# Opening of the kernel: three issuing queues, sums of squares on TensorE, one joint root, first step 512 wide

## The chip, the cores and the metric

The kernel runs on one core of a Trainium2 chip. The metric is the device time of one execution in microseconds: 1518.89 us before, the median of 3 runs (1516.44 to 1520.34). A profiled execution took 1518.84 us, of which the profile's span covers 1517.1 us. All times in the texts below count from the start of that span.

## The reference

A two-layer backbone block. There are two token streams of 256 tokens each, 1024 channels wide: the latents x and the context ctx. What the change touches is the very beginning of layer 0:

```python
mod_x = (jax.nn.silu(c) @ w_mod[l] + b_mod[l])[:, None, :]
mod_c = (jax.nn.silu(c_ctx) @ w_mod[l] + b_mod[l])[None, None, :]
hc = _modulate(xc, g_pre_mix[l], sc1, cc1)
h = _modulate(x, g_pre_mix[l], sx1, cx1)
proj = h @ w_in
# _modulate(x, g, shift, scale) = _rms_norm(x, g) * (1 + scale) + shift
# _rms_norm(x, g) = x * rsqrt(mean(x * x) + EPS) * g
```

So each token needs the sum of its 1024 squares and a reciprocal root, each channel needs a shift and a scale that come from a product of the conditioning vector with `w_mod`, and then the projections begin. All else (Fourier mixing, two attentions, a convolution, gates, the MLP, and layer 1) follows on these results and isn't changed.

## The kernel before, in words

Activations are held channel-major: x is eight tiles of 128 channels x 512 tokens, stream 0 (the latents) in columns 0 to 255 and stream 1 (the context) in columns 256 to 511. A matrix product in full precision is done as three passes over parts: each operand is split into a high part (a cast, on ACT) and a low part (a subtraction, on DVE), and `mm3` (L147) issues high x high (L149), high x low (L150) and low x high (L151).

The opening of layer 0 is `conv_proj` (L760). It takes eight steps, one per block k of 128 input channels, and in each step six output tiles (six PSUM banks: four "mm", one "tp", one "o") take 3 matmuls each, 18 in all, 512 columns wide from step 1 on (`wide`, L748). Step k needs the modulated block k of both streams (`entry`, L1236, and `modulate_tile`, L362: a multiply on DVE, L367, the high part on ACT, L132, the low part on DVE, L133), its weights (`raw`, 384 KB, loaded by SP and split at L126 and L127), and the shifts and scales of block k. These come from `mods_pe` (L246): a load of 1 MB (`boot`, a ring of six tiles), sixteen matmuls at L256, a copy on ACT (L259), four small matmuls at L261 and an addition on DVE (L264). Block k+2 is done behind step k.

Step 0 has a function of its own, `start` (L1211). For each stream in turn it squares eight x tiles on ACT (L1220) and adds them up on DVE (L1222), sums over the partitions with products against a column of ones on PE (`rstd_add`, L317), takes the root on DVE with Newton steps (`rsqrt_cols`, L175), spreads it over the partitions with products against the identity on PE (`rstd_rows`, L359) and copies the result to SBUF. Stream 0's root, modulation and half of step 0 (256 columns) come first; then those of stream 1.

The loads of the opening are issued in `load_x` (L230) from SP's queue, in this order: stream 0's eight x tiles, the first block of `w_mod`, two tables, the first weights, stream 1's eight x tiles. Two more tables are issued from ACT's queue in `setup` (L186). One DMA completes on one of a few semaphores that are taken in turn, so a later issue can wait for an earlier landing.

The order of instructions on each engine is fixed before the run by a planner. It goes by priorities and by estimated times: work within `high_priority` goes ahead, and work that is ready by its estimate can be put ahead of older work that isn't.

Of the kernel before, what the change touches and what calls it, by code (L numbers as in the profile page):

```python
# [9 lines left out]
F = mybir.dt.float32  # L10
R = mybir.dt.float32r
I32 = mybir.dt.int32
BF = mybir.dt.bfloat16
AF = mybir.ActivationFunctionType
ALU = mybir.AluOpType
AX = mybir.AxisListType
ORDER = mybir.DependencyInfo(mybir.DependencyClass.NoSync, mybir.DependencyReason.DATA)
PSUM = bass.MemoryType.PSUM

P = 128  # L20
D = 1024
KT = 8
L = 256
T = 512
DEPTH = 2
EPS = 1e-6
# [9 lines left out]
C_COS, C_SIN, C_ID, C_ONE = 0, 256, 512, 640  # L36
C_HSEL = 768
C_RSEL = 770
NCONST = C_RSEL + 2
# [41 lines left out]
class Body:  # L81
# [20 lines left out]
    def new(self, name, shape, dtype=F, pool=None, space=None):  # L102
        if space is not None:
            pool = getattr(self, "psum", None)
            if pool is None:
                pool = self.psum = self.ec(self.tc.tile_pool(name="psum", bufs=1, space=PSUM))
        return (pool or self.const).tile(shape, dtype, tag=name, name=name)
# [39 lines left out]
    def mm3(self, out, w, x, start, stop, shared=False):  # L147
        nc = self.nc
        i = nc.tensor.matmul(out, w[0], x[0], start=start, stop=False, skip_group_check=shared)  # L149
        nc.tensor.matmul(out, w[0], x[1], start=False, stop=False, skip_group_check=shared)  # L150
        nc.tensor.matmul(out, w[1], x[0], start=False, stop=stop, skip_group_check=shared)  # L151
        return i

    def mms(self, out, passes, start, stop):
        for i, (w, x) in enumerate(passes):
            self.nc.tensor.matmul(out[:w.shape[-1]], w, x, start=start and i == 0, stop=stop and i == len(passes) - 1)  # L156
# [26 lines left out]
            for o, q, h in cols:  # L183
                self.hold = nc.vector.scalar_tensor_tensor(o, q, 1.5, o, ALU.add, ALU.mult).ins.name

    def setup(self):  # L186
        nc, a, new = self.nc, self.a, self.new
        c = self.consts = new("consts", [P, NCONST])
        ccol, th = new("ccol", [P, KT, 2]), new("cth", [P, KT, 2])
        nc.scalar.dma_start(ccol, a["ccol"])  # L190
        nc.scalar.dma_start(c[:, C_ID:], a["consts"][:, C_ID:])
        self.cos, self.sin = c[:, C_COS:C_COS + L], c[:, C_SIN:C_SIN + L]
        self.ident, self.ones = c[:, C_ID:C_ID + P], c[:, C_ONE:C_ONE + P]
        self.hsel = c[:, C_HSEL:C_HSEL + 2]
        self.rsel = c[:, C_RSEL:C_RSEL + 2]
        nc.scalar.activation(th, ccol, AF.Tanh, scale=0.5)
        self.scol = new("scol", [P, KT, 32])
        nc.vector.memset(self.scol, 0.0)
        nc.vector.scalar_tensor_tensor(th, th, 1.0, ccol, ALU.add, ALU.mult)
        nc.vector.tensor_scalar(self.scol[:, :, 0:2], th, 0.5, None, ALU.mult)  # L200

        self.mods = new("mods", [P, DEPTH, 48, 2])
        self.coef = new("coef", [P, DEPTH, 4, KT, 2])
        self.st4 = self.ring("st4", 16, [P, 4])
        self.st8 = [new(f"st8_{i}", [P, 8]) for i in range(4)]
        self.st32 = [new(f"st32_{i}", [P, 32]) for i in range(4)]
# [20 lines left out]
        for l in range(DEPTH):  # L227
            nc.vector.tensor_scalar(self.dwh[:, l], self.vec[:, l, V_DW:V_DW + 3 * TAPS].rearrange("p (j t) -> p j t", j=3), 0.5, None, ALU.mult)

    def load_x(self):  # L230
        self.vec = self.new("vecs", [P, DEPTH, NVEC])
        self.bmod = self.new("bmod", [P, DEPTH, 48])
        with self.tc.high_priority(WPRIO):
            for k in range(KT):
                self.nc.sync.dma_start(self.x[k][:, :L], self.a["xT"][0, k])
            self.first = {0: self.boot()}
            self.nc.sync.dma_start(self.first[0], self.a["wmod0"][0])
            self.nc.sync.dma_start(self.bmod, self.a["bmod"])
            self.nc.sync.dma_start(self.vec, self.a["vecs"])
            raw0 = self.raw()[:, :768]  # L240
            self.nc.sync.dma_start(raw0, self.a["wuc"][0, 0])
            for k in range(KT):
                self.nc.sync.dma_start(self.x[k][:, L:], self.a["xT"][1, k])
        return raw0

    def mods_pe(self, c):  # L246
# [651 lines left out]
    def attention_part(self, l, n):  # L898
        tc = self.tc
        ns = self.ns = n // L  # L900
        if l == 0:
            with tc.tile_pool(name="boot", bufs=1, reuse_waits="tile") as pool:
                self.boot = self.ring("boot", 6, [P, 2 * D], F, pool)
                raw0 = self.load_x()
                self.setup()
                cbanks = self.conv_proj(l, n, raw0)
            self.setup_late()
        else:
            cbanks = self.conv_proj(l, n)
        with ExitStack() as ctx:  # L910
            pool = ctx.enter_context(tc.tile_pool(name=f"mix{l}", bufs=1, reuse_waits="tile"))
            new = lambda name, shape, dtype=F: self.new(f"{name}", shape, dtype, pool)
# [25 lines left out]
            banks = [self.ps() for _ in range(4)]  # L938
# [151 lines left out]
            for s in range(ns):  # L1090
                sl = slice(s * L, (s + 1) * L)
                acc = self.stat(l)
# [116 lines left out]
                self.chain = self.norm_step(l, 3, ya, acc, s, 1.0 / D, None, (l + 1, 0), "mm")  # L1209

    def start(self, banks, raw0):  # L1211
        self.rs0 = self.tmp("l")
        sls = [slice(s * L, (s + 1) * L) for s in range(2)]
        two = []
        for s in range(2):
            acc = self.rstd_bank(L, "s" if s else "o")
            sm = self.tmp("l")[:, :L]
            for k in range(KT):
                sq = self.tmp("g")[:, :L] if k else sm
                self.nc.scalar.activation(sq, self.x[k][:, sls[s]], AF.Square)  # L1220
                if k:
                    self.nc.vector.tensor_tensor(sm, sm, sq, op=ALU.add)  # L1222
            self.rstd_add(acc, sm, 0, 0)
            two.append(self.rstd_sum(acc, L, 1.0 / D))
            if s == 0:
                self.mods_pe(0)
                self.nc.scalar.copy(self.rs0[:, sls[0]], self.rstd_rows(*two[0], L))
                self.entry(0, (0,))
                w = self.chunk(raw0, (1, 768), first=False)
                self.mods_pe(1)  # L1230
        self.wide(None, self.h, sls[0], banks, 0, w)
        self.nc.scalar.copy(self.rs0[:, sls[1]], self.rstd_rows(*two[1], L))
        self.entry(0, (1,), False)
        self.wide(None, self.h, sls[1], banks, 0, w)

    def entry(self, k, streams, coefs=True):  # L1236
        if coefs:
            self.coefs(0, 0, k, k + 1)
        for s in streams:
            self.modulate_tile(0, 0, s, k, self.rs0[:, s * L:(s + 1) * L])  # L1240

# [43 lines left out]
WPRIO = 4000  # L1285
# [104 lines left out]
```

## Time and profile before

| | |
|---|---|
| median of 3 runs | 1518.89 us |
| profiled execution | 1518.84 us |
| its span | 1517.1 us |
| TensorE (PE) busy | 1454.5 us, 96% |
| VectorE (DVE) busy | 1192.3 us, 79% |
| ScalarE (ACT) busy | 802.5 us, 53% |
| GpSimd (POOL) busy | 123.0 us, 8% |
| one x tile of one stream | 128 KB, 16 of them |
| one block of `w_mod` (boot) | 1024 KB |
| weights of one step (raw) | 384 KB |
| tables consts, vecs, bmod, ccol | 130, 137, 48 and 8 KB |

The page gives each engine's busy time, then the span in 40 slices with a digit for the busy tenths of each, then the chain of work that ended last. In a row of a timeline the first number is the start in us, the second the duration, then engine, line, operation, what is written and read, and the count; in brackets stands the idle time before it and what ended it. A name that ends in q is an engine's queue, which issues DMAs. Rows that merge several instructions give the stretch that they cover.

### The profile page before, as it was taken

What the parts mean: (1) busy time and instruction counts of PE and PEld (TensorE: products, weight loads), DVE (VectorE), ACT (ScalarE), POOL (GpSimd) and SP (SyncE); (2) the same over time, 40 slices, a digit from 0 to 9 for tenths busy, and PEclk for the clock granted to TensorE, in tenths of its full rate; (3) what the DMA queues carried; (4) which work ended last, traced back from release to release, by engine and by line L of the source; (5) the groups of instructions that cost most, each with busy time, mean ns of one, the idle gap of its engine ahead of it and who ended that gap; (6) DMA issues with size and microseconds to landing.
All of it is one profiled execution on the core that took longest, in us unless ns stands there. A gap on an engine that the chain in (4) does not pass through costs nothing.

```text
span 1517.1 us, 25021 instructions
## 1 busy us (share of the span) xinstructions
PE 1454.5 (96%) x9242; PEld 1297.4 (86%) x9242; DVE 1192.3 (79%) x2689; ACT 802.5 (53%) x1584; POOL 123.0 (8%) x165
## 2 busy tenths in 40 slices
PE   5999999999999999899999999989998999899997
PEld 4787788878787899898889999978798999899886
DVE  5699998888889959748975577889998976675565
ACT  3334665555554346753443335553775775577643
POOL 0100000002121002201110011120000110000000
PEclk9999999999999999999999999999999999999999
DMA  8522222413335554666776565362232445466552
GB/s 310 163 71 80 67 66 67 139 56 125 113 122 156 181 181 141 233 196 209 242 254 196 181 223 181 112 214 73 86 108 84 140 132 177 130 203 196 168 191 98
DMA packets 74010, 230.02 MB, mean 152 GB/s; under 512 B 8480, under 2 KB 17184, under 8 KB 72608
## 3 DMA queue, kind: packets, MB, share of 16 engines
q1 hardware_dynamic: 60192, 181.10, 37.1%
q0 software_dynamic: 13408, 47.19, 9.6%
q8 instruction: 72, 1.18, 0.3%
q14 instruction: 50, 0.41, 0.1%
q10 hardware_dynamic: 288, 0.14, 0.0%
HBM read 227.35 MB, written 1.05 MB: 151 GB/s over the span
## 4 chain that ended last, share of the span: by engine, by line
PE 79%; DVE 10%; ACT 4%; DMA 3%; issue 2%; POOL 0%; SPq 0%; DVEq 0%; ACTq 0%; POOLq 0%
PE ps_mm L149 20%; PE ps_mm L150 19%; PE ps_mm L151 19%; PE ps_s L438 3%; DVE wl L127 2%; PE ps_s L156 2%; PE ps_tp L438 1%; PE ps_o L438 1%; PE ps_tp L550 1%; ACT wh L126 1%; PE ps_o L156 1%; PE ps_s L149 1%; PE ps_s L150 1%; PE ps_s L151 1%; PE ps_o L150 1%
## 5 line engine op out<-in xcount | busy, mean ns | idle before, releaser
L126 ACT CAST wh<-raw 128x1024 fp32r<-128x1024 f32 (+3 forms) x283 | 259.9, 919 | 312.7 <-PE ps_mm L150 168.3
L127 DVE TENSOR_TENSOR wl<-raw,wh 128x1024 fp32r<-128x1024 f32 (+3 forms) x283 | 304.7, 1078 | 137.5 <-ACT wh L126 135.4
L149 PE MATMUL ps_mm<-h,wh 128*128 128x512 f32 (+2 forms) x996 | 344.4, 348 | 8.1 <-ACT h L132 3.9
L151 PE MATMUL ps_mm<-h,wl 128*128 128x512 f32 (+2 forms) x996 | 345.1, 347 | 4.7 <-DVE wl L127 4.5
L150 PE MATMUL ps_mm<-h,wh 128*128 128x512 f32 (+2 forms) x996 | 343.5, 345 | 0.0
L149 PEld LDWEIGHTS ps_mm<-h,wh 128*128 128x128 f32 x996 | 190.0, 192 | 32.4 <-ACT h L132 4.1
L151 PEld LDWEIGHTS ps_mm<-h,wl 128*128 128x128 f32 x996 | 191.1, 192 | 29.3 <-DVE wl L127 7.9
L150 PEld LDWEIGHTS ps_mm<-h,wh 128*128 128x128 f32 x996 | 191.0, 192 | 21.8 <-issue 0.8
L127 DVE TENSOR_TENSOR wlx<-raw,whx 128x1024 fp32r<-128x1024 f32 (+2 forms) x85 | 93.9, 1106 | 34.6 <-ACT whx L126 34.4
L799 DVE SCALAR_TENSOR_TENSOR cy<-cv,half_dw,cy 128x512 f32<-128x512 f32 (+1 forms) x180 | 102.7, 610 | 0.2
L149 PE MATMUL ps_mm<-h,whx 128*128 128x256 f32 (+2 forms) x336 | 98.4, 294 | 4.3 <-ACT tf L516 2.5
L126 ACT CAST whx<-raw 128x1024 fp32r<-128x1024 f32 (+2 forms) x85 | 80.9, 953 | 40.9 <-PE ps_mm L150 19.9
L287 DVE SCALAR_TENSOR_TENSOR tl<-wm,srow 128x1024 bf16<-128x1024 f32 x80 | 97.6, 1220 | 0.8
L150 PE MATMUL ps_mm<-h,whx 128*128 128x256 f32 (+2 forms) x336 | 97.9, 292 | 0.0
L151 PE MATMUL ps_mm<-h,wlx 128*128 128x256 f32 (+2 forms) x336 | 97.0, 292 | 0.0
L151 PE MATMUL ps_mm<-r,wl 128*128 128x256 f32 (+1 forms) x260 | 86.3, 332 | 1.6 <-DVE wl L127 1.6
L149 PE MATMUL ps_mm<-r,wh 128*128 128x256 f32 (+1 forms) x260 | 86.5, 333 | 0.1
L150 PE MATMUL ps_mm<-r,wh 128*128 128x256 f32 (+1 forms) x260 | 86.0, 331 | 0.0
L126 ACT CAST hs<-hid 128x256 fp32r<-128x256 f32 x96 | 38.6, 407 | 70.9 <-PE ps_o L438 39.5
L149 PEld LDWEIGHTS ps_mm<-h,whx 128*128 128x128 f32 x336 | 63.8, 190 | 6.3 <-ACT tf L516 2.7
L127 DVE TENSOR_TENSOR hs<-hid,hs 128x256 fp32r<-128x256 f32 x96 | 41.8, 439 | 34.5 <-ACT hs L126 33.9
L855 POOL TENSOR_TENSOR x<-x,tg 128x512 f32<-128x512 f32 (+1 forms) x32 | 36.8, 1149 | 354.9 <-DVE tg L853 293.8
(398 smaller groups left out, 3538.7 us busy)
## 6 DMA issues: line engine op xcount, KB each, us to landing
raw<-in_wff SPq DMA_DIRECT2D x135, 512.0 KB, 4.2
raw<-in_wcol SPq DMA_DIRECT2D x88, 512.0 KB, 3.5
wm<-in_wmodT POOLq DMA_DIRECT2D x56, 512.0 KB, 4.1
wmg<-in_wmodT POOLq DMA_DIRECT2D x24, 512.0 KB, 3.8
raw<-in_wout SPq DMA_DIRECT2D x24, 512.0 KB, 3.9
boot<-in_wmod SPq DMA_DIRECT2D x8, 1024.0 KB, 7.4
raw<-in_wuc SPq DMA_DIRECT2D x16, 384.0 KB, 3.3
raw<-in_wdv SPq DMA_DIRECT2D x8, 512.0 KB, 3.7
```

The costliest lines, as they stand in the source:

```text
L126: nc.scalar.copy(hi, src)
L127: return nc.vector.tensor_tensor(lo, src, hi.bitcast(F), op=ALU.subtract)
L149: i = nc.tensor.matmul(out, w[0], x[0], start=start, stop=False, skip_group_check=shared)
L150: nc.tensor.matmul(out, w[0], x[1], start=False, stop=False, skip_group_check=shared)
L151: nc.tensor.matmul(out, w[1], x[0], start=False, stop=stop, skip_group_check=shared)
L156: self.nc.tensor.matmul(out[:w.shape[-1]], w, x, start=start and i == 0, stop=stop and i == len(passes) - 1)
L287: i = nc.vector.scalar_tensor_tensor(self.junk, w, 1.0, self.srow[:, s, :], ALU.mult, ALU.mult, accum_out=self.mods[:, l, c, s:s + 1])
L438: self.nc.tensor.matmul(banks[t][i][:, c], x[q][:, tok], w[j][:, a:b], start=start and j + q == 0, stop=stop and q == 1, skip_group_check= ...
L550: nc.tensor.transpose(ps[:, i * P:(i + 1) * P], p[:, i * P:(i + 1) * P], self.ident)
L799: nc.vector.scalar_tensor_tensor(y3, src, w, y3, ALU.mult, ALU.add)
L855: eng.tensor_tensor(mg, mg, th, op=ALU.add)
```

## The change

The loads go out from three queues: stream 0's x tiles, then the weights, from SP; stream 1's x tiles from POOL; the tables and the first block of `w_mod` from ACT. Squares of stream 0 are taken on ACT, those of stream 1 on DVE, and nothing is added up there: each squared tile goes to PE, where products against the column of ones accumulate over the eight tiles in four columns of one PSUM bank, two for each stream. One root is taken for all four columns, spread over 512 columns and copied once; then both streams are modulated and step 0 is done 512 wide. PE also gets fourteen matmuls of 512 columns on a zeroed bfloat16 tile whose result nobody reads: six at the beginning and one behind the sums of each k. The small tiles of the setup move to the pool of the opening, and the setup's four small operations get a high priority.

```diff
+    def load_x(self, pool):
+        nc = self.nc
...
         with self.tc.high_priority(WPRIO):
+            nc.gpsimd.memset(self.warm, 0.0)
+            self.first = {0: self.boot()}
+            nc.scalar.dma_start(self.ccol, self.a["ccol"])
+            nc.scalar.dma_start(self.consts[:, C_ID:], self.a["consts"][:, C_ID:])
+            nc.scalar.dma_start(self.bmod, self.a["bmod"])
+            nc.scalar.dma_start(self.vec, self.a["vecs"])
+            nc.scalar.dma_start(self.first[0], self.a["wmod0"][0])
             for k in range(KT):
-                self.nc.sync.dma_start(self.x[k][:, :L], self.a["xT"][0, k])
-            self.first = {0: self.boot()}
-            self.nc.sync.dma_start(self.first[0], self.a["wmod0"][0])
-            self.nc.sync.dma_start(self.bmod, self.a["bmod"])
-            self.nc.sync.dma_start(self.vec, self.a["vecs"])
+                nc.sync.dma_start(self.x[k][:, :L], self.a["xT"][0, k])
+            for k in range(KT):
+                nc.gpsimd.dma_start(self.x[k][:, L:], self.a["xT"][1, k])
             raw0 = self.raw()[:, :768]
-            self.nc.sync.dma_start(raw0, self.a["wuc"][0, 0])
-            for k in range(KT):
-                self.nc.sync.dma_start(self.x[k][:, L:], self.a["xT"][1, k])
+            nc.sync.dma_start(raw0, self.a["wuc"][0, 0])
...
     def start(self, banks, raw0):
+        nc = self.nc
         self.rs0 = self.tmp("l")
-        sls = [slice(s * L, (s + 1) * L) for s in range(2)]
-        two = []
-        for s in range(2):
-            acc = self.rstd_bank(L, "s" if s else "o")
-            sm = self.tmp("l")[:, :L]
+        junk, bank, out = self.ps("s"), self.ps("o"), self.ps("tp")
+        sums = bank[:, T - 4:]
+
+        def keep_warm():
+            nc.tensor.matmul(junk, self.warm[:, :P], self.warm, start=True, stop=True)
+
+        for i in range(6):
+            keep_warm()
+        head = None
+        with self.tc.high_priority(2 * WPRIO):
             for k in range(KT):
-                sq = self.tmp("g")[:, :L] if k else sm
-                self.nc.scalar.activation(sq, self.x[k][:, sls[s]], AF.Square)
-                if k:
-                    self.nc.vector.tensor_tensor(sm, sm, sq, op=ALU.add)
-            self.rstd_add(acc, sm, 0, 0)
-            two.append(self.rstd_sum(acc, L, 1.0 / D))
-            if s == 0:
-                self.mods_pe(0)
-                self.nc.scalar.copy(self.rs0[:, sls[0]], self.rstd_rows(*two[0], L))
-                self.entry(0, (0,))
-                w = self.chunk(raw0, (1, 768), first=False)
-                self.mods_pe(1)
-        self.wide(None, self.h, sls[0], banks, 0, w)
-        self.nc.scalar.copy(self.rs0[:, sls[1]], self.rstd_rows(*two[1], L))
-        self.entry(0, (1,), False)
-        self.wide(None, self.h, sls[1], banks, 0, w)
+                for s in range(2):
+                    x = self.x[k][:, s * L:(s + 1) * L]
+                    sq = self.tmp("fa"[s])[:, :L]
+                    if s == 0:
+                        nc.scalar.activation(sq, x, AF.Square)
+                    else:
+                        nc.vector.tensor_tensor(sq, x, x, op=ALU.mult)
+                    for t in range(2):
+                        i = nc.tensor.matmul(sums[:, 2 * s + t:2 * s + t + 1], sq[:, t * P:(t + 1) * P], self.ones[:, 0:1],
+                                             start=head is None, stop=k == KT - 1, skip_group_check=True)
...
+                keep_warm()
+        self.mods_pe(0)
+        v, r, q, h = (self.st4() for _ in range(4))
+        nc.vector.tensor_scalar(v, sums, 1.0 / D, EPS, ALU.mult, ALU.add)
+        self.rsqrt(r, v, q, h)
+        nc.scalar.copy(self.rs0, self.rstd_rows(out, r, T))
+        self.entry(0, range(2))
+        w = self.chunk(raw0, (1, 768), first=False)
+        self.mods_pe(1)
+        self.wide(None, self.h, slice(0, T), banks, 0, w)
```

`rsqrt` (L166) is the root that is now called: two operations, then three times three, each on all columns at once.

## Rows read from the trace of the kernel before

**Rows 1.** The page: busy time of the engines; busy tenths of the DMA engines.

```profile
PE 1454.5 (96%) x9242; PEld 1297.4 (86%) x9242; DVE 1192.3 (79%) x2689; ACT 802.5 (53%) x1584; POOL 123.0 (8%) x165
...
DMA  8522222413335554666776565362232445466552
```

**Rows 2.** The chain that ended last, its first 36 us: start, duration, what.

```profile
4.50 7.79 DMA boot<-in_wmod
12.32 1.98 PE ps_s L256 x16
...
20.21 0.21 PE ps_mm L150
...
31.35 0.12 PE ps_mm L151
...
33.41 0.43 PE ps_mm L149
```

**Rows 3.** Timeline: DMA issues on SP's queue, and later ones on POOL's.

```profile
6.55 7.58 SPq L243 DMA_DIRECT2D x<-in_xT  x8
...
13.80 0.33 SPq L243 DMA_DIRECT2D x<-in_xT  x1
...
62.79 2.13 POOL L708 DMA_DIRECT2D r<-in_csl  x4 [9.38 <-PE ps_s L256]
```

**Rows 4.** DMA issues (count, size, us to landing), and a wait of SP's queue.

```profile
x<-in_xT SPq DMA_DIRECT2D x1, 128.0 KB, 2.7
...
r<-in_csl POOLq DMA_DIRECT2D x4, 256.0 KB, 4.5
...
SPq L243 <- DMA boot<-in_wmod: 2.0, 1, 2.0
```

**Rows 5.** Stretches: length, busy time per engine, granted clock, DMA share, GB/s.

```profile
2.00:14.00 12.00, 2.69 (x20) 1.51 (x20) 5.69 (x29) 4.31 (x10) 0.00 (x0) 1.00 0.90 280
10.00:12.00 2.00, 0.00 (x0) 0.00 (x0) 1.78 (x15) 0.00 (x0) 0.00 (x0) 1.00 0.95 352
...
24.00:28.00 4.00, 2.15 (x21) 1.37 (x14) 2.87 (x18) 1.43 (x4) 0.00 (x0) 0.97 1.00 407
28.00:31.00 3.00, 3.00 (x11) 1.97 (x12) 2.33 (x5) 1.45 (x3) 0.00 (x0) 0.50 1.05 430
...
38.13:43.94 5.81, 5.81 (x40) 4.16 (x39) 3.40 (x9) 2.02 (x4) 0.00 (x0) 1.00 0.69 250
```

**Rows 6.** Timeline: products of the root, of a steady step, of a block.

```profile
14.19 1.22 PE L359 MATMUL ps_o<-consts,st 128*128 128x128 f32 x4
...
22.57 0.85 PE L317 MATMUL ps_s<-consts,tl 128*128 128x1 f32 x4
...
25.30 0.71 PE L359 MATMUL ps_s<-consts,st 128*128 128x128 f32 x4 [0.41 <-DVE st L184]
...
34.75 0.35 DVE L264 TENSOR_SCALAR mods<-ps_s,bmod 128x2 f32<-128x2 f32 x2 [4.31 <-PE ps_s L261]
...
39.13 0.50 PE L149 MATMUL ps_mm<-h,wh 128*128 128x512 f32 x1
...
43.94 1.07 PE L256 MATMUL ps_s<-boot,scol 128*32 128x256 f32 x16
```

**Rows 7.** Timeline: DVE and ACT operations that the sum is made from.

```profile
4.35 0.42 DVE L1222 TENSOR_TENSOR tl<-tl,tg 128x256 f32<-128x256 f32 x1 [0.60 <-ACT tg L1220]
...
9.94 0.16 DVE L327 TENSOR_SCALAR st<-ps_o 128x2 f32<-128x2 f32 x1 [1.11 <-PE ps_o L317]
...
11.58 0.28 DVE L184 SCALAR_TENSOR_TENSOR st<-st,st 128x1 f32<-128x1 f32 x2
...
35.33 0.88 DVE L367 SCALAR_TENSOR_TENSOR ta<-x,coef,tl 128x256 f32<-128x256 f32 x2
...
35.85 0.91 ACT L132 ACTIVATE h<-ta,mods 128x256 fp32r<-128x256 f32 x2 [2.01 <-DVE ta L367]
...
70.07 0.60 ACT L782 ACTIVATE tf<-ps_mm 128x512 f32<-128x512 f32 x1 [2.13 <-PE ps_mm L151]
```

More of the change, by code (lines that the diff above doesn't have):

```diff
@@ L184, in rsqrt_cols, with setup @@
                 self.hold = nc.vector.scalar_tensor_tensor(o, q, 1.5, o, ALU.add, ALU.mult).ins.name
-    def setup(self):
+    def setup(self, pool):
         nc, a, new = self.nc, self.a, self.new
[L188 to L191, printed above, removed]
+        c, ccol = self.consts, self.ccol
+        th = new("cth", [P, KT, 2], F, pool)
         self.cos, self.sin = c[:, C_COS:C_COS + L], c[:, C_SIN:C_SIN + L]
@@ L195, in setup @@
         self.rsel = c[:, C_RSEL:C_RSEL + 2]
[L196 to L200, printed above, removed]
+        with self.tc.high_priority(2 * WPRIO):
+            nc.scalar.activation(th, ccol, AF.Tanh, scale=0.5)
+            self.scol = new("scol", [P, KT, 32], F, pool)
+            nc.vector.memset(self.scol, 0.0)
+            nc.vector.scalar_tensor_tensor(th, th, 1.0, ccol, ALU.add, ALU.mult)
+            nc.vector.tensor_scalar(self.scol[:, :, 0:2], th, 0.5, None, ALU.mult)
         self.mods = new("mods", [P, DEPTH, 48, 2])
@@ L228, in setup_late @@
             nc.vector.tensor_scalar(self.dwh[:, l], self.vec[:, l, V_DW:V_DW + 3 * TAPS].rearrange("p (j t) -> p j t", j=3), 0.5, None, ALU.mult)
-    def load_x(self):
+    def load_x(self, pool):
+        nc = self.nc
         self.vec = self.new("vecs", [P, DEPTH, NVEC])
         self.bmod = self.new("bmod", [P, DEPTH, 48])
+        self.consts = self.new("consts", [P, NCONST])
+        self.ccol = self.new("ccol", [P, KT, 2], F, pool)
+        self.warm = self.new("warm", [P, T], BF, pool)
         with self.tc.high_priority(WPRIO):
-            for k in range(KT):
-                self.nc.sync.dma_start(self.x[k][:, :L], self.a["xT"][0, k])
-            self.first = {0: self.boot()}
-            self.nc.sync.dma_start(self.first[0], self.a["wmod0"][0])
-            self.nc.sync.dma_start(self.bmod, self.a["bmod"])
-            self.nc.sync.dma_start(self.vec, self.a["vecs"])
+            nc.gpsimd.memset(self.warm, 0.0)
[5 more added lines that the diff above has]
+            nc.scalar.dma_start(self.first[0], self.a["wmod0"][0])
+            for k in range(KT):
+                nc.sync.dma_start(self.x[k][:, :L], self.a["xT"][0, k])
+            for k in range(KT):
+                nc.gpsimd.dma_start(self.x[k][:, L:], self.a["xT"][1, k])
             raw0 = self.raw()[:, :768]
-            self.nc.sync.dma_start(raw0, self.a["wuc"][0, 0])
-            for k in range(KT):
-                self.nc.sync.dma_start(self.x[k][:, L:], self.a["xT"][1, k])
+            nc.sync.dma_start(raw0, self.a["wuc"][0, 0])
         return raw0
@@ L903, in attention_part @@
                 self.boot = self.ring("boot", 6, [P, 2 * D], F, pool)
-                raw0 = self.load_x()
-                self.setup()
+                raw0 = self.load_x(pool)
+                self.setup(pool)
                 cbanks = self.conv_proj(l, n, raw0)
@@ L1231, in start @@
-        self.wide(None, self.h, sls[0], banks, 0, w)
-        self.nc.scalar.copy(self.rs0[:, sls[1]], self.rstd_rows(*two[1], L))
-        self.entry(0, (1,), False)
-        self.wide(None, self.h, sls[1], banks, 0, w)
-    def entry(self, k, streams, coefs=True):
-        if coefs:
-            self.coefs(0, 0, k, k + 1)
+        junk, bank, out = self.ps("s"), self.ps("o"), self.ps("tp")
+        sums = bank[:, T - 4:]
+        def keep_warm():
+            nc.tensor.matmul(junk, self.warm[:, :P], self.warm, start=True, stop=True)
@@ new lines, in start @@
+        for i in range(6):
+            keep_warm()
+        head = None
+        with self.tc.high_priority(2 * WPRIO):
+            for k in range(KT):
+                for s in range(2):
[8 more added lines that the diff above has]
+                                             start=head is None, stop=k == KT - 1, skip_group_check=True)
+                        if head is not None and k == 0:
+                            self.tc.add_manual_dep(i.ins, head, ORDER, reason="bank clear first")
+                        head = head or i.ins.name
+                keep_warm()
@@ L1239, in entry @@
+        self.mods_pe(0)
[7 more added lines that the diff above has]
+        self.wide(None, self.h, slice(0, T), banks, 0, w)
+    def entry(self, k, streams):
+        self.coefs(0, 0, k, k + 1)
         for s in streams:
```

## The prediction

> **What bounds the kernel now.** I read the page first, then the chain of waits of the first 36 us, then the table of stretches, then single instructions there. Over the whole span TensorE is busy 96% and the DMA engines are mostly not [rows 1]; only in the first slice are they at 8 tenths. So a microsecond won at the opening is won at the end, if the first dense step starts earlier and nothing starves it after. What I follow is one mark: the start of the second projection step, at 33.41 in the chain [rows 2]. From there on a step takes 5.81 us of PE without a gap (38.13 to 43.94, PE busy 5.81 of them) with 250 GB/s of transfers beside it, less than the 352 and 407 of earlier stretches [rows 5]. Later steps are copies of this one, so whatever moves the mark moves the end.
>
> The chain up to the mark [rows 2]: the first modulation block (1 MB) is issued behind eight x tiles at 4.50 and takes 7.79; its products begin at 12.32; around 20 PE does step 0 for stream 0 alone, the sums of stream 1 wait behind it (22.57) [rows 6], a second root follows, and stream 1's half of step 0 runs from 28 on. There the granted clock reads 0.50, the level of 1.2 GHz, after a stretch 24 to 28 in which PE had 2.15 us of work [rows 5]. The clock column reads 1.00 before that, but matmuls of 256 columns start 0.21 apart at 20.21 and 0.12 apart at 31.35 [rows 2]; I go by the spacing and take PE as running at half speed until about 23.
>
> **The change part by part.** Sum against the profiled execution: 1518.84 us, of which 1517.1 is the span; the median of the three runs is 1518.89, so the two are interchangeable.
>
> *Loads.* Before, SP issues all 16 x tiles, stream 1 behind the block: its eight issues take 7.58 us [rows 3], one of them held 2.0 us by the block's landing [rows 4]. The last x tile is issued at 13.80 and lands 2.7 later, at 16.5 [rows 3, 4]. Now stream 1 goes out from POOL, whose issues cost 0.53 each (2.13 for four) [rows 3], eight done by about 5.5; nothing else that the opening needs stands on POOL. Needed before the last sum: x 2.10 MB, the block 1.05, small tables 0.33, in all 3.48 MB, since the three queues run at once and the block on ACT's queue takes its share. Between 2 and 14 us the transfers ran at 280 GB/s [rows 5]: 2 + 12.4 = 14.4 us for the last x tile. Below: at 352 (10 to 12 us) 11.9. Above: if SP's next loads (0.39 and 1.05 MB) pass a lagging stream 1, 4.92 MB, 19.6.
>
> *Sums of squares.* The additions on DVE go (14 of about 0.43, [rows 7]), DVE squares stream 1 instead. Squares of the last tile 0.43, its two one-column products 0.85 (22.57) [rows 6]: 15.7. ACT's squares of stream 0 run three tiles ahead and are hidden as long as x arrives slower than 0.43 per tile, which 14.4 says.
>
> *The joint root.* Before, 1.92 us for two columns (9.94 to 11.86) [rows 7]. Now twelve instructions, one behind the other; dependent ones start 0.19 to 0.20 apart there: 2.2. To 17.9. The first modulation block's products (1.07 to 1.98) are hidden under it; if they weren't, see rival C.
>
> *Rows of the root.* Four products instead of two: 0.71 at the fast and 1.22 at the slow spacing for two [rows 6], so 1.2 to 2.1; I take 1.5, to 19.4. The copy to SBUF is 512 wide, 0.60 as a like copy [rows 7]: 20.0. Then both streams' modulation, as in a steady step from 35.33 to 36.76, 1.43 [rows 7]: PE can start step 0 at 21.4.
>
> *Step 0, 512 wide.* A steady step without the block behind it is 39.13 to 43.94, 4.8, four small products of the block before it included [rows 6], which stand here too. The engine comes to it from a thin stretch like that of 24 to 28; before, 3.1 us passed at half speed then [rows 5], which would cost half of that, 1.6; with the extra products in the gap I take 0.8. To 27.0. The next block's products take 1.0 [rows 6], so the mark is at 28.0 instead of 33.4: a gain of 5.4.
>
> *Added and hidden.* Fourteen warming products (512 columns, some 0.21 to 0.43 each, from the spacings above doubled) stand in PE while it waits for x. Without that cover, they would cost up to 8 x 0.43 = 3.4, and this is in rival D. The memset of their operand costs POOL well below one DMA issue. Tables moved to other queues land earlier, which nobody waits for.
>
> *What is late next.* The second block follows on SP behind x and the first weights: 4.92 MB is through by 19.6 at 280 GB/s, before step 0 starts at 21.4. The third follows 1.44 MB later, 3.5 us at 407 and 5.1 at 280, so at 24.7 at the latest, and is wanted at 27.0. So no transfer takes over the path.
>
> A rule that speaks against the change: the Trainium skill, "DMA: Bandwidth & Descriptors", section "Issuing engines are not separate DMA queues", says that transfers started from several engines share the same 16 DMA engines and interleave, so that spreading them saves only issue time. The trace agrees so far as the mean busy share was already 0.90 between 2 and 14 us with nearly everything on SP [rows 5]; its result is rival A.
>
> Sum: 1518.84 - 5.4 = 1513.4 us.
>
> **Rivals.**
>
> A. *The transfer isn't won.* Stream 1 on POOL is overtaken by what SP issues after its own x tiles; the last x lands at 19.6, 5.2 later than forecast, gain 0.2: 1518.6. For it: DMA share 0.90, and large rows beside 1 KB rows; POOL's transfers of 256 KB took 4.5 us to land [rows 4]. Against: both x queues are issued within a microsecond of each other. The same page, section "Queues, rings and completion order", has every DMA engine go round the queues packet by packet, which would make this worse with larger packets; no row here shows packets of three queues at once.
>
> B. *More is won.* Transfers reach 352 GB/s (11.9, 2.5 earlier), and the warming products keep PE at the fast level: sums 0.35 less, rows 0.3 less, step 0 0.8 less. Gain 5.4 + 2.5 + 0.65 + 0.8 = 9.4: 1509.4. For it: 352 and 407 GB/s were reached once larger rows were in flight; against: x rows alone ran near 280 and below.
>
> C. *The planner puts the first block's chain ahead of the root* on DVE, as it is written before it. Then the root waits for the block's products, 1.07, and from their end to that of the addition, 1.7 (33.41 to 35.10) [rows 2, 6], with projection products in between; of these 2.8 I take 2.2, gain 3.2: 1515.6. Before, it reordered freely by readiness, which speaks against.
>
> D. *Slower: sums bound by PE at half speed.* A tile pair costs four one-column products (twice 0.85) and one warming product 0.43: 2.1 us. From about 5 us, eight take until 22.1, against 15.7; rows 2.1 (0.6 more); step 0 starts at half speed for 3.1 us (0.7 more than counted): 7.7 lost against the forecast, 1521.1; with all of step 0 (18 x 0.43, 2.1 more than counted) and its block (1.98, 0.9 more) at half speed 10.0 lost, 1523.4. It decides when the sums end after 15.7 + 5.4 = 21.1. For it: PE worked nearly gap-free from 12.32 to about 16 and still had the slow spacing at 20.21 [rows 2]. Against: the dense work from 28 on [rows 5] brought the fast spacing by 31.35 [rows 2].
>
> **How the numbers follow.** Forecast 0.42 (own range 1511 to 1516), A 0.15, B 0.23, C 0.10, D 0.10. Some 0.3% (4.6 us) is what a measurement can tell from no change. Faster by more: 0.28 of the forecast, which stands only 0.8 beyond that bound, all of B, 0.02 of C: 0.53. Slower by more: 0.07 of D and 0.02 of A, whose upper end I don't know: 0.09. The rest, 0.38, within. The range reaches from just below B to past A, 1508.5 to 1520.0, and leaves out D and a little of B.
>
> **What would show it.** Right: last x tile landed by 13 to 16 us; the root's first instruction near 15.7; step 0's first product of 512 columns near 21.4; step 1's at 26 to 30, and the same 5.81 us steps after. Loads wrong: the wait before the last squares is on x and ends near 19 (A) or near 12 (B). Order wrong: DVE's first modulation addition stands ahead of the root (C). Clock wrong: sums packed without a gap at 2 us per tile pair, the granted clock at 0.50 in step 0 (D). The whole prediction fails if steps after the second are no longer 5.81 us, or if the gain at the mark is there and isn't at the end.

## The result and the profile after

The kernel after takes 1530.28 us (median of 6 runs, 1526.66 to 1531.12), the kernel before beside it 1519.12 (6 runs): ratio 1.0077, 95% interval 1.0058 to 1.0095. It is slower, where 1513.4 was forecast. The profiled execution took 1530.87 us, its span 1529.0. The mark (start of step 1), 33.41 in the chain of before [rows 2], is at 43.08 in the chain after, 9.7 us later instead of 5.4 earlier. So most of the 11.9 us between the two spans arises in the opening.

First the page of the kernel after, engines and DMA; it answers to [rows 1]:

```profile
PE 1475.6 (97%) x9294; PEld 1311.9 (86%) x9294; DVE 1189.3 (78%) x2665; ACT 799.0 (52%) x1575; POOL 129.0 (8%) x174
...
DMA  7432222322444554766776565362223445466552
```

TensorE has 21.1 us more busy time than before (1454.5), and 18.1 of it stand ahead of the mark: 35.74 us busy up to 42.94, before 17.67 up to 33.34. Of these, 6.05 are the warming products, which ran while TensorE had nothing else to do. The chain of waits after shows most of the rest (start, duration, what; it answers to [rows 2]):

```profile
3.11 9.05 DMA boot<-in_wmod
...
12.30 1.03 PE ps_s L262 x2
13.33 1.80 PE ps_o L1239 x8
15.13 1.01 PE ps_s L262 x8
16.14 3.50 PE ps_o L1239 x16
19.64 1.00 PE ps_s L262 x6
20.64 6.92 PE ps_o L1239 x32
27.56 0.99 PE ps_s L262 x2
28.55 0.95 PE ps_s L267 x4
29.49 1.89 PE ps_s L262 x14
...
31.89 1.03 PE ps_s L267 x4
...
33.76 2.09 PE ps_tp L365 x8
...
38.04 1.20 PE ps_mm L149 x4
...
43.08 0.35 PE ps_mm L149
```

This is to be read from the top. L262 are the products of the first modulation block, L1239 the one-column products of the sums. The chain does not begin at x. It begins at the first block (1 MB), which lands at 12.16, and the one-column products follow it: 1.80 + 3.50 + 6.92 = 12.2 us of them, with 3.0 us of block products between. The sums end at 27.56.

The timeline after, TensorE and then VectorE (start, duration, engine, line, operation; in brackets the idle time before it and what ended it):

```profile
1.32 6.05 PE L1224 MATMUL ps_s<-warm 128*128 128x512 bf16 x14 [1.32 <-POOL warm L237]
7.21 0.50 PE L1239 MATMUL ps_o<-consts,tf 128*128 128x1 f32 x4
7.58 0.58 PE L1239 MATMUL ps_o<-consts,ta 128*128 128x1 f32 x4
12.30 1.03 PE L262 MATMUL ps_s<-boot,scol 128*32 128x256 f32 x2 [4.14 <-DMA boot<-in_wmod]
...
27.60 0.16 DVE L1247 TENSOR_SCALAR st<-ps_o 128x4 f32<-128x4 f32 x1 [8.33 <-PE ps_o L1239]
29.59 0.35 DVE L270 TENSOR_SCALAR mods<-ps_s,bmod 128x2 f32<-128x2 f32 x2 [1.43 <-PE ps_s L267]
33.01 0.22 DVE L270 TENSOR_SCALAR mods<-ps_s,bmod 128x2 f32<-128x2 f32 x1 [2.21 <-PE ps_s L267]
33.54 0.16 DVE L173 SCALAR_TENSOR_TENSOR st<-st,st 128x4 f32<-128x4 f32 x1
```

The planner put all 14 warming products first, then pair 0 of the sums, and directly behind it products of a block that had not landed. TensorE stood still for 4.14 us with further squares of x waiting to be summed. On VectorE the root (27.60 to 33.70) has the additions of blocks 0 and 1 (L270) in it, and waits 1.43 and 2.21 us for the products that these need.

Stretches after (length, busy time of PE, PEld, DVE, ACT, POOL, granted clock, DMA share, GB/s), answering to [rows 5]:

```profile
8.20:12.30 4.10, 0.00 (x1) 0.03 (x2) 1.98 (x10) 0.15 (x1) 0.00 (x0) 0.79 1.01 381
12.30:27.50 15.20, 15.20 (x73) 12.72 (x73) 2.14 (x4) 2.85 (x6) 0.00 (x0) 0.50 1.03 417
27.50:33.70 6.20, 4.86 (x25) 2.60 (x24) 2.32 (x18) 0.37 (x1) 0.00 (x0) 0.50 0.18 74
```

TensorE was idle from 8.2, then filled every one of the next 15.2 us, and the granted clock read 0.50 (the level of 1.2 GHz) all that time. Pair 0 had run at the other level: a product is two instructions here, the first four of pair 0 take 0.37 us until the next four start (7.21, 7.58); in the chain, four take 6.92 / 8 = 0.87 in the stretch at 0.50. Steady steps are as before: 48.33 to 54.14 in the chain, 5.81 us.

### The profile page after: what moved, and what is told of

Same layout as the page of the kernel before. It is cut to its first block, busy times and chain, and to the rows that moved or that the text cites. A ratio compares the mean times of both kernels' runs of the same rounds, so it can differ in the third digit from the quotient of the medians.

```text
span 1529.0 us, 25085 instructions
## 1 busy us (share of the span) xinstructions
PE 1475.6 (97%) x9294; PEld 1311.9 (86%) x9294; DVE 1189.3 (78%) x2665; ACT 799.0 (52%) x1575; POOL 129.0 (8%) x174
## 4 chain that ended last, share of the span: by engine, by line
PE 81%; DVE 11%; ACT 4%; DMA 3%; issue 2%; POOL 0%; DVEq 0%; ACTq 0%; POOLq 0%
PE ps_mm L149 20%; PE ps_mm L150 19%; PE ps_mm L151 19%; PE ps_s L444 3%; DVE wl L127 3%; PE ps_s L156 2%; PE ps_tp L444 1%; PE ps_o L444 1%; PE ps_tp L556 1%; ACT wh L126 1%; DVE tl L315 1%; PE ps_o L150 1%; PE ps_o L151 1%; PE ps_s L149 1%; PE ps_o L149 1%
```

## Experiments

The theories, as the expectations name them. S: the sums are late on TensorE, by the planner's order and by half speed. R: the torn root on VectorE is what costs. L: the new loads cost. C: TensorE's clock decides, and the warming products should stand between the pairs. Orders are pinned with the order edges that the kernel already uses. Times are medians; "x" is the landing of the last x tile, the other columns are from the profile of each run. The mark in the table is the start of step 1's first product in the timeline. In before and in e9 to e12 block 2's products (1.1 us) stand directly ahead of that mark, in the others they are done before step 0; e7 has block 3's done by its mark too, so that its mark overstates its delay. Before and e7 do step 0 in two halves and have two starts; their sums and rows are those of stream 1. The ratios go by the runs of before taken beside each: 1519.12 beside after, 1517.65 beside e1 to e4, 1517.05 beside e5 to e8, 1517.83 beside e9 to e12.

| run | us (runs) | ratio to before, 95% | x | sums end | rows start | step 0 | mark |
|---|---|---|---|---|---|---|---|
| before | 1517.65 (25) | | 16.46 | 23.41 | 25.30 | 18.56 / 27.79 | 33.34 |
| after | 1530.28 (6) | 1.0058 to 1.0095 | 13.75 | 27.56 | 33.76 | 38.04 | 42.94 |
| e1 | 1518.84 (10) | 0.9994 to 1.0023 | 13.52 | 19.03 | 25.27 | 29.27 | 34.34 |
| e2 | 1526.2 (4) | 1.0038 to 1.0084 | 13.41 | 27.14 | 32.34 | 37.26 | 41.86 |
| e3 | 1521.0 (10) | 1.0008 to 1.0035 | 13.38 | 18.18 | 25.07 | 29.99 | 36.14 |
| e4 | 1520.44 (10) | 1.0012 to 1.0035 | 13.25 | 23.16 | 27.30 | 30.67 | 35.73 |
| e5 | 1516.23 (10) | 0.9972 to 0.9997 | 13.50 | 18.05 | 21.08 | 27.74 | 32.40 |
| e6 | 1519.47 (10) | 0.9991 to 1.0023 | 13.51 | 18.52 | 23.49 | 29.23 | 34.13 |
| e7 | 1519.52 (10) | 1.0000 to 1.0029 | 13.22 | 30.56 | 33.05 | 27.84 / 36.60 | 40.46 |
| e8 | 1527.69 (5) | 1.0037 to 1.0076 | 13.94 | 27.83 | 34.02 | 38.31 | 43.44 |
| e9 | 1513.42 (12) | 0.9964 to 0.9988 | 13.57 | 17.15 | 19.38 | 23.97 | 29.75 |
| e10 | 1511.95 (8) | 0.9950 to 0.9976 | 13.43 | 17.11 | 19.49 | 23.89 | 29.67 |
| e11 | 1517.24 (12) | 0.9986 to 1.0010 | 13.75 | 18.52 | 21.80 | 25.99 | 31.74 |
| e12 | 1515.83 (12) | 0.9973 to 0.9995 | 17.24 | 21.57 | 23.80 | 28.01 | 34.04 |

**e1, order on TensorE alone.** Every block product stands behind the last product of the sums.

```diff
+            if self.summed:          # in mods_pe, for each block product i
+                self.tc.add_manual_dep(i.ins, self.summed, ORDER, reason="after the sums")
...
+        self.summed = i.ins.name     # in start, behind the loop over k
```

> Edit: the products of the modulation blocks are ordered behind the last sum of squares on TensorE, nothing else. Theory S (the sums are late on TensorE: the planner put products of block 0, which wait for that block's landing at 12.2 us, behind the first pair, and the seven other pairs then take 1.73 us each at half speed with three more lots of block products among them): the 4.1 us of idle time and 3 us of products between the sums go, the sums end at 20.3 if the remaining pairs still run at half speed and near 15 if they don't, instead of 27.5; step 1 begins 7 to 12 us earlier than at 42.9 and the time is 1518 to 1523. Rival L (the three queues delay the loads): the last x tile landed at 13.7 anyway, and the order on TensorE changes nothing, 1530. Rival R (the root is late because additions of the blocks stand in it on VectorE, 6.1 us for 2.2): these stay, so at most 3 us, 1527 to 1530.

Measured: sums end 19.03 for 27.56, mark 34.34 for 42.94; 1518.84 us, no longer different from before. This one order is worth 8.5 us at the sums and 8.6 at the mark. Theory S holds. TensorE in e1:

```profile
18.04 0.99 PE L1241 MATMUL ps_o<-consts,ta 128*128 128x1 f32 x4
18.96 2.78 PE L262 MATMUL ps_s<-boot,scol 128*32 128x256 f32 x22
...
25.27 1.79 PE L367 MATMUL ps_tp<-consts,st 128*128 128x128 f32 x8 [0.65 <-DVE st L173]
```

The sums still end 5.5 us behind the last x tile, since from 8.9 on a pair takes 1.7 us of TensorE. The root is torn as in after: the rows wait for it until 25.27.

**e2, order on VectorE alone.** The blocks' additions stand behind the root.

```diff
+            if self.rooted:          # in mods_pe, for each addition o
+                self.tc.add_manual_dep(o.ins, self.rooted, ORDER, reason="after the root")
```

> Edit: the additions that finish the modulation blocks are ordered behind the root on VectorE, the order on TensorE stays. Rival R (the torn root costs 3.9 us): 1526.4. Theory S: the root ends near 29.8 instead of 33.7, but TensorE still has the products of block 1 and four small ones ahead of the root's rows until 32.9, so step 1 begins about 0.9 us earlier, 1529.4.

Measured: the root now runs in one piece, but the mark moves by only 1.1 us, to 41.86. VectorE in e2, end of the root and the next additions:

```profile
29.14 0.16 DVE L173 SCALAR_TENSOR_TENSOR st<-st,st 128x4 f32<-128x4 f32 x1
...
32.59 0.22 DVE L270 TENSOR_SCALAR mods<-ps_s,bmod 128x2 f32<-128x2 f32 x1 [2.99 <-PE ps_s L267]
```

The root ends 4.4 us earlier than in after (29.30 for 33.70), but the rows start only 1.4 earlier (32.34), behind both blocks' products on TensorE. The time, 1526.2, is the one that R named (1526.4), but its interval holds S's 1529.4 as well; the mark, which S put 0.9 earlier and R's price would put 3.9 earlier, decides. R as the main cause falls.

**e3, both orders; e4, both orders and the last eight warming products each behind its pair.**

```diff
-                keep_warm()
+                keep_warm(i.ins.name)   # e4 only: an edge to the pair's last product
```

> Edit: both orders of the two other experiments. Theory S: as with TensorE's order alone within 1 us, since the products of blocks 0 and 1 stand behind the sums and ahead of the rows: end of the sums + 10.5 us to step 0 + 4.9 to step 1, so 35.7 for sums that end at 20.3 (1522 to 1523) and 30.4 for 15 (1517.5). Rival R: both gains add up, 3 us better than TensorE's order alone. Rival L: no change beyond 0.5 us.

> Edit: both orders, and each of the eight warming products that belong behind a pair is ordered behind that pair's sums (the planner had put all 14 at the beginning, where they ended at 7.2). Theory C (the cost is the clock: one-column products keep TensorE at 1.2 GHz, products of 512 columns between them lift it): a pair takes 1.3 us, the sums follow the x tiles and end near 16, what follows runs at full speed, step 1 begins near 27.5, 1515. Theory S without C: the pairs stay at half speed and take 2.16 us with their warming product, the sums end near 22 to 24, step 1 begins at 37 to 39, 1524 to 1527, worse than both orders alone.

Measured: e3's root ends at 21.10, 4.1 us before e1's, and its mark is 1.8 later. The first products of its step 0:

```profile
29.99 2.08 PE L149 MATMUL ps_mm<-h,wh 128*128 128x512 f32 x4 [1.00 <-ACT h L132]
```

In e3 the rows wait behind the products of blocks 0 and 1 (25.07), and step 0 starts at half speed: its first four products of 512 columns take 2.08 us, those of e1 1.20. In e4 step 0 runs at the fast spacing (its first two in 0.73), but the sums end only at 23.16: two of their products (four instructions) took 0.7 to 0.9 from 5.36 to the end, with the warming products between. The granted clock reads 1.00 in that stretch of e4 (15.0 to 23.5), and in e8 over sums as slow as those of after (12.4 to 27.8), so the spacing, not that column, tells the speed there. So neither reached what was expected: e3's mark is 1.8 off e1's where S said within 1, and e4 has the late sums of S without C but a mark 1.3 earlier than S said. From step 0 on the clock costs or gives back some 1 us (step 0 to mark 6.15 in e3, 5.07 in e1). It is not what made the kernel slow, as e1's sums run at the same half speed. What half speed itself costs in the sums no run isolates, since e4's products between the pairs did not lift it.

**e5, sums on VectorE; e6, as e1 with the rows first.** e5 squares both streams on ScalarE, adds them up on VectorE, and has 4 one-column products at the end. Block 1's products stand behind the rows in both.

```diff
+                    sq = self.tmp("fa"[s])[:, :L] if k else sm[s]
+                    nc.scalar.activation(sq, self.x[k][:, s * L:(s + 1) * L], AF.Square)
+                    if k:
+                        nc.vector.tensor_tensor(sm[s], sm[s], sq, op=ALU.add)
...
+        self.summed = self.lastrow.ins.name   # behind the rows: block 1 on
```

> The kernel after with the squares of both streams on ScalarE, added up on VectorE, so that TensorE has 4 one-column products at the end in place of 32 along the way; block 1's products stand behind the rows of the root, and its additions behind the root. Theory S (the opening is late because TensorE carries the sums): sums end 0.5 to 3 us after the last x tile (13.4 to 13.8), so 14.5 to 16.6, block 0's products standing ahead of them; root to 18.7, rows to 20.8, step 0 at 23 to 24, the later end if it waits for a block's load that stands ahead of it; mark (start of step 1) 28 to 29, 14 us before that of the kernel after, time 1513 to 1516. Theory L' (ScalarE and VectorE can't keep pace with x either): sums end 19 or later, mark 32 or later, 1517 or more. Theory C (what counts is TensorE's clock): after the idle wait in front of the sums the engine comes to step 0 at half speed, 18 products by 0.43 for 0.23, mark 31 to 33.

> The order on TensorE alone (32 one-column products ahead of every block's products) as in e1, and the rows of the root ahead of block 1's products. Theory S: sums end near 19 as in e1, root 2.2 to 3.2, rows to 24, step 0 at 26.5 and mark at 31 to 32, 2 to 3 us before e1's 34.3; time 1516 to 1517. If block 1's products ahead of the rows had cost nothing (the root is what is late): mark 34, time as e1, 1519.

Measured: e5 is the first version below before (1516.23, ratio 0.9972 to 0.9997), yet its mark is 3.4 us past the 28 to 29 expected; e6's is 34.13, not 31 to 32. Both numbers fit a rival named beforehand: e5's mark theory C's 31 to 33, e6's mark and time the case that block 1's products cost nothing (34, 1519). The traces speak against both: e5's step 0 runs at the fast spacing (its first two products in 0.73), and e6's rows start 1.8 earlier than e1's. Both runs have their rows earlier than e1 and lose it again in front of step 0. ScalarE of e6 shows it, and e5 has the same copy at 25.09:

```profile
27.27 0.37 ACT L267 COPY tf<-ps_s 128x256 f32<-128x256 f32 x1 [1.08 <-PE ps_s L262]
27.54 0.83 ACT L126 CAST wh<-raw 128x768 fp32r<-128x768 f32 x1
...
28.27 0.91 ACT L132 ACTIVATE h<-ta,mods 128x256 fp32r<-128x256 f32 x2
```

The operand of step 0 (h) stands behind the copy of block 1, which waits for TensorE, and behind a cast of the next weights. An edge on one engine moves the wait to the next one.

**e7, the loads alone, in the kernel before; e8, the kernel after without its 14 warming products.**

```diff
-                self.nc.sync.dma_start(self.x[k][:, L:], self.a["xT"][1, k])
+                nc.gpsimd.dma_start(self.x[k][:, L:], self.a["xT"][1, k])   # e7, and the block on ACT's queue
...
-                keep_warm()                                                # e8
```

> The kernel before with the loads of the kernel after alone (three queues), sums, roots and steps as before. Theory S: the loads are no part of what was lost; last x lands near 13.5 for 16.5, and the mark moves from 33.3 by 0 to 3 us earlier, the smaller if the additions on VectorE, which ended at 21.7, and not x are what the second root waited for; 1515 to 1518. Theory L (the three queues cost the opening, by the block or the weights that come later): mark later than 34, 1519 or more.

> The kernel after without its 14 warming products; everything else as there, block 0's products between the sums' as the planner puts them. Theory S: the warming products stand in 1.3 to 7.2 us and only pair 0 waits for them, while all later pairs wait behind block 0's load; sums end at 27 to 28 as before, mark 42 to 43, 1529 to 1531. Theory C (the products hold up the sums, or spend the fast clock too early): sums end 2 us or more earlier, mark 40 or less, 1527 or less.

Measured for e7: x lands 3.2 us earlier, and the mark comes 7.1 us later; 1519.52, at the edge of what can be told from before. By the number that is theory L, and a load is in it. At the start of the last step, where the same blocks are done, e7 is 5.3 behind (72.41 for 67.09). ScalarE and then TensorE in e7:

```profile
14.21 0.83 ACT L126 CAST wh<-raw 128x768 fp32r<-128x768 f32 x1 [8.26 <-DMA raw<-in_wuc]
...
21.79 1.93 PE L260 MATMUL ps_s<-boot,scol 128*32 128x256 f32 x16 [0.84 <-DVE mods L268]
23.66 1.22 PE L363 MATMUL ps_o<-consts,st 128*128 128x128 f32 x4
...
27.84 1.22 PE L149 MATMUL ps_mm<-h,wh 128*128 128x256 f32 x4 [2.31 <-ACT h L132]
```

With other loads the planner wrote another order. On ScalarE the cast of the first weights stands ahead of all squares but the first three, and waits 8.26 us for weights that land at 14.19 (13.79 in before). So this is the fault of the kernel after once more, on another engine. The last tile of stream 0, which this kernel needs first, also lands later: 13.22 for 7.87. Stream 0's sums end at 20.1 for 9.9, the products of blocks 1 and 2 stand ahead of its rows, and its half of step 0 starts at 27.84 for 18.56. e8: sums end 27.83, mark 43.44. The warming products cost nothing and brought nothing; 1527.69 is 1.3 below the expected range, the mark 0.4 above its own.

**e9, the order written out.** e5, with block 0's small products behind the sums, its additions and the first weights' split behind the root, block 1's copy behind step 0's operand, and blocks 2 on behind step 0. **e10** adds 4 warming products between sums and rows; **e11** has e9's order with the sums of the kernel after (32 one-column products, stream 1 squared on VectorE, block 0's products behind them); **e12** has e9 with the loads of before.

```diff
+            if c == 0:    # small products m of block 0
+                self.tc.add_manual_dep(m.ins, self.summed, ORDER, reason="after the sums")
+        if c == 1:        # copy cp of block 1
+            self.tc.add_manual_dep(cp.ins, self.lasth, ORDER, reason="after the first modulation")
...
+        self.summed = self.lastmm   # behind step 0: block 2 on
```

> As e5 (squares on ScalarE, additions on VectorE, 4 one-column products at the end), with the order written out further: block 0's small products behind the sums', its additions and the split of the first weights behind the root on VectorE, block 1's copy behind step 0's operand on ScalarE, block 2's products and later ones behind step 0. Theory S (what was forecast for the change, mark 28.0, is reached once the products of the sums and of the blocks stand in the right place): sums end 17.6, root 19.8, rows 21.9, step 0 at 24, mark 28.5 to 29.5, time 1512 to 1513.5. Theory L' (a load is late next: the weights of step 0 or block 1): step 0 waits on a DMA, mark 31 or later, 1515 or more. Theory C (clock): the rows and step 0 at half speed, mark 31 to 32.

> As e9, with 4 more warming products (0.43 each) in TensorE's wait between the sums and the rows. Theory C (dense work ahead of step 0 brings the fast spacing earlier): rows 1.2 for 2.1, block 1's products 1.0 for 1.9, mark 0.8 to 2 earlier than e9's. If TensorE's speed there doesn't decide: mark as e9's within 0.3; if they hold up the rows, up to 1 later.

> As e9 in its order, but with the sums as in the kernel after: 32 one-column products on TensorE, DVE's products for stream 1's squares, block 0's products behind them all. Theory S: sums end at 18.5 to 19, block 0's products then 3 us, root to 21.2, rows to 24, step 0 near 26, mark 30.7 to 31.3, 1.5 to 2.5 later than e9's; time 1514 to 1516. If the one-column products weren't a cost of their own (order alone): mark as e9's, 29.

> As e9 with the loads of the kernel before: both streams of x, the first block and the first weights on SP's queue alone. Loads worth what they save (last x 16.5 for 13.5, 3.0 us): sums end near 19.5 to 20, mark 31 to 32, time 2 to 3 us above e9's. If the later part (root, blocks) hides them: mark within 0.5 of e9's.

Measured: e9 takes 1513.42 us, 0.9964 to 0.9988 of before, and is at its mark at 29.75, 13.2 us ahead of the kernel after. Its opening:

```profile
15.14 0.42 DVE L1246 TENSOR_TENSOR tl<-tl,ta 128x256 f32<-128x256 f32 x1
15.29 1.87 PE L1250 MATMUL ps_o<-consts,tl 128*128 128x1 f32 x8 [1.31 <-DVE tl L1246]
17.19 0.16 DVE L1257 TENSOR_SCALAR st<-ps_o 128x4 f32<-128x4 f32 x1 [1.63 <-PE ps_o L1250]
19.38 2.08 PE L375 MATMUL ps_tp<-consts,st 128*128 128x128 f32 x8 [1.37 <-DVE st L175]
...
23.97 0.73 PE L151 MATMUL ps_mm<-h,wh 128*128 128x512 f32 x2 [0.65 <-ACT h L132]
28.75 1.07 PE L264 MATMUL ps_s<-boot,scol 128*32 128x256 f32 x16
29.75 0.50 PE L151 MATMUL ps_mm<-h,wh 128*128 128x512 f32 x1
```

Up to the copy of the rows every piece now follows its predecessor within 0.2 us; the modulation starts 0.4 behind the copy. The last addition ends 2.0 us behind the last x tile. TensorE of e11 (rows, step 0) and of e12 (sums):

```profile
21.80 2.06 PE L375 MATMUL ps_tp<-consts,st 128*128 128x128 f32 x8
...
25.99 0.73 PE L151 MATMUL ps_mm<-h,wh 128*128 128x512 f32 x2 [0.46 <-ACT h L132]
```

```profile
20.55 1.01 PE L1250 MATMUL ps_o<-consts,tl 128*128 128x1 f32 x4 [5.48 <-DVE tl L1246]
```

e9's mark is 0.25 us above the expected range, its time in it. e11's mark is 2.0 us behind e9's, as expected (its time, 1517.24, is 1.2 above the range): with everything else in place, the sums on TensorE cost 2 us at the mark. e12's mark is 4.3 behind, more than expected, though its time is 2.4 above e9's as expected: its x lands 3.7 later, and its sums end 4.4 later. e10's mark is 0.1 us from e9's, so theory C falls; that its median is 1.5 us lower has no counterpart in the opening and stays unexplained, the intervals overlap.

## Why the prediction was wrong

The step that failed is *Sums of squares*: "Squares of the last tile 0.43, its two one-column products 0.85: 15.7". It took for granted that TensorE has nothing else to do and keeps pace with x. The sums ended at 27.56, 11.9 us later. e1 gives the parts: without block products between, 19.0 (18.5 in e6 and e11), so 8.5 to 9 us are the order, above all the wait of 4.14 for a block and 3.0 of its products; the other 3 are TensorE's own pace, 1.7 us per tile pair at half speed from about 9 us on. That pace was priced in rival D. The place of the block's products was priced nowhere: the prediction hid them under the root, although they are written ahead of it and the block's bytes were counted as landed with the last x; rival C looked for the planner's choice on VectorE alone. Why the planner put them between the sums, against the priority of the sums, no run shows.

The other terms, one by one:

- *Loads*, 14.4 for the last x tile: 13.75. Right, and rival A falls. Their worth is 4.3 us at the mark and 2.4 in the time (e12 against e9), but only where the order lets it through (e7). The Trainium skill, "DMA: Bandwidth & Descriptors", section "Issuing engines are not separate DMA queues", grants several issuing engines only the issue time, usually small. By that, little was to be had; here 3.7 us were (13.57 in e9, 17.24 in e12). Most of it can be one wait on the issuing queue, as SP's was held for 3.2 us by the block's landing in e12. So issue time is not always small; the measurement decides.
- *The joint root*, 2.2: alone it takes 2.1 (17.19 to 19.32 in e9). In after it took 6.1, for rival C's reason and with two blocks instead of one. Undoing that (e2) gives 1.1 us at the mark, half of C's price, because the rows waited for TensorE anyway.
- *Rows* 1.5: 2.1, at half speed, the upper bound. Copy and modulation 2.0: 2.2 (35.83 to 38.04).
- *Step 0* with the four small products, 5.6: 4.9 (38.04 to 42.94), at the fast spacing from 39.5 on; over-priced by 0.7. The next block's 1.0 fell away, as its products had run before step 0. With these the terms close: 28.0 + 11.9 + 3.9 + 0.6 + 0.2 - 0.7 - 1.0 = 42.9.
- *Warming products hidden*: right (e8), and of no use where they stood. The memset of their operand was to be well below one DMA issue on POOL; it took 0.52, where eight issues took 4.43. The dense work they did was followed by the wait to 12.30, and the clock was at half again.
- *What is late next*: no load held up step 0, as forecast. The first block held up the sums, which no step had.
- *Rival D* had the side and the engine, with sums at 22.1 from 2.1 us per pair. The pair costs 1.7, but D knew nothing of the block, so its 1521.1 to 1523.4 fell short by 7 to 9.
- *The mark gives the end*: only within some 4 us. After is 9.6 behind before at the mark and 11.9 in the span, e9 3.6 and 7.7 ahead, e12 0.7 behind and 2.2 ahead. The later program isn't the reason: from 135 us on before and after run the same instructions in the same order on every engine (one matmul record aside). The distance between them falls to 4 us by about 910 and is back at 10 by 1040. There the granted clock differs, 1.00 in before (first row) and 0.95 in the matching stretch of after (second). Why one execution is granted less stays open. The interval of the ratio, 8.8 to 14.4 us, holds the 9.6 of the mark.

```profile
920.00:1050.00 130.00, 120.83 (x857) 112.32 (x857) 110.86 (x255) 68.34 (x131) 19.08 (x21) 1.00 0.46 143
```

```profile
925.00:1060.00 135.00, 124.97 (x847) 116.49 (x846) 110.60 (x255) 66.55 (x130) 19.08 (x21) 0.95 0.44 137
```

The kernel that the prediction described, with its order put right, is e11: sums on TensorE, mark 31.74 for 28.0, time no different from before (0.9986 to 1.0010). So with its order right the change as described gains 1.6 us at the mark, and nothing that the time shows. The sum comes near to e9, which is another kernel, with the additions left on VectorE. Its mark is 29.75: sums 1.45 later, rows, copy and modulation 1.1 longer, step 0 and the next block 0.8 shorter. That its time, 1513.42, meets the forecast is partly chance: it won some more after the mark, and before took 1517.83 beside it, not 1518.89.

## What to carry to other kernels

Where a planner or a list fixes the order on each engine, a sum of durations along the wanted path is not yet a forecast: ask for every engine on that path which other ready-to-be-placed work may be put in front, and when the input of that work lands. One instruction that waits for a late load stops all that stands behind it on its engine, and an edge on one engine only hands the wait to the next (e2, e5, e6). Moving sums to TensorE because it is idle there pays only if it is really idle and fast at that moment; here additions on VectorE kept pace with x, and the one-column products did not. An early mark is worth what it shows only if the same work is done by it (e7), and single executions can differ by some us behind it.

## What the runs showed of the hardware

A one-column fp32 product seems to cost what its weights cost. In e3 groups of two products, four instructions with a weight load of 128 columns each, start at 7.50, 7.95, 8.39 and 8.84, 0.45 us apart, and later at 12.06, 12.92, 13.77 and 14.62, 0.85 apart, for a single column each. In e9, at a granted clock of 0.50, instructions with such weights start 0.21 apart whether they have 1, 2 or 128 columns (from 15.52, 17.01 and 19.75 on), while sixteen with weights of 32 columns, and 256 columns each, take 1.94 together (from 21.38). The Trainium skill, "TensorE: Matmul & The Clock Gate", section "LDWEIGHTS (loading the stationary operand)", gives a load its number of columns over 1.2 in ns, which is 107 for 128, and names no clock. The fast spacing agrees (0.11 per instruction); at a granted clock of 0.50 it is 0.21, which that rule doesn't give.

TensorE without a gap of more than some hundredths, filled mostly with such products, still read 0.50: 15.2 us in after, and 6.95 us in e11, the first fence. In e9, the second fence, rows of 128 columns and block 1's products of 256 run at 0.50. The rise to 1.00 comes at 23.6, in the 0.65 us of idle time ahead of step 0. In e3 the same rows and block products were followed by 1.00 us of idle time, and the clock stayed at 0.50 until 33.2, well into step 0.

```profile
11.50:18.45 6.95, 6.92 (x33) 6.91 (x33) 1.78 (x6) 2.04 (x4) 0.00 (x0) 0.50 1.03 412
```

```profile
19.40:21.40 2.00, 2.00 (x11) 1.78 (x11) 1.13 (x4) 0.83 (x1) 0.00 (x0) 0.50 1.01 415
21.40:24.00 2.60, 1.95 (x18) 0.61 (x17) 2.31 (x6) 1.57 (x4) 0.00 (x0) 0.58 1.04 423
24.00:29.00 5.00, 5.00 (x28) 3.88 (x32) 2.71 (x9) 1.41 (x4) 0.00 (x0) 1.00 1.01 410
```
